# Two-layer hybrid decoder on one core: the memory's load, the pieces of the weight subtraction, and the order of layer 1's side work

## The chip, the cores and the metric

The kernel runs on one core of one Trainium2 chip. A core has five engines that work at the same time and wait for one another through semaphores: PE (TensorE, matrix products), DVE (VectorE), ACT (ScalarE), POOL (GpSimd) and SP (SyncE, which here only starts transfers). Transfers between main memory and the on-chip memory (SBUF) run on 16 DMA engines; SP and ACT each have a queue from which they are started in order. Products land in PSUM, a small second memory of eight banks. The metric is the device time of one execution in microseconds; lower is better. The number given for a kernel is the median of its runs.

## The reference

The input is x (512 tokens by 1024 channels) and a memory of 256 tokens. Each of two layers adds three things to x: a mixer, a cross-attention into the memory, and a gated feed-forward block with a short convolution. Only the mixers differ, and cut to what matters here they are:

```
layer 0:  xn = rmsnorm(h);  q, k, v, p = split(xn @ ev_w_in)
          a = block-sparse attention of 8 heads (q, k, v)
          b = per group g of 4: trailing mean of p over w = 2, 4, 8, 16 tokens, minus p, @ pool_w[g]
          h += concat(a, b) @ ev_w_out
layer 1:  z, qkv, gate, b_raw, a_raw = split(rmsnorm(h) @ od_w_in)
          u, v = split(gelu(z));  v = layernorm(v);  c = u * (tril(W) v + bias)      # spatial gate
          q, k, v = silu(short convolution of qkv), per head normed                  # 4 heads
          d = gated delta rule over chunks (triangular solve in a chunk, a scan over chunks)
          h += concat(c, d * silu(gate)) @ od_w_out
each:     mem_n = rmsnorm(mem);  k, v = split(mem_n @ wkv);  h += softmax(q k') v @ wo
          h += (silu(g) * up) @ down       # after a causal convolution of width 3
```

## The kernel before

x is held transposed, channels on the 128 partitions, as eight tiles of 128 by 512. Every product is made in three passes: both operands are split into a high part rounded to a shorter format and a low remainder, and PE adds high x high, high x low and low x high (`mm3`, lines 115 to 118). So a product of a 1024-deep weight block with 512 tokens is 8 k-steps of three matmuls.

**Weights.** `fetch` (line 120) starts a 512 KB transfer from SP's queue into one of three raw buffers. `wload` (line 125) makes the high part with a copy on ACT (line 108) and the low part, raw minus high, with one subtraction over all 1024 columns on POOL (line 109); the high parts have three buffers, the low parts two. So POOL can be one product ahead of PE and then waits until PE gives a buffer back. `parts=2` at the start lets the first three weights go in two halves, each a copy and a subtraction. In the last products of the kernel the subtraction is given to DVE (`sub=nc.vector`).

**Order of the work.** PE's order is written by hand in both mixers (`manual_schedule`), in layer 1 POOL's as well; elsewhere the framework orders the engines by its own estimate when the program is built. The tool for writing PE's order is a queue of generators: `later` appends work, and `fill(n)` lets PE do n units of it, a unit being one k-step of three matmuls with 512 columns (half a unit for the 256 tokens of the memory). `fill` stands wherever PE would otherwise wait for a chain on DVE or ACT. The amounts are the constants FILL_QT, FILL_AV, FILL_INV, FILL_LEV and FILL_SCAN at the top.

**Start.** `setup` (line 296) starts, on SP, the eight tiles of x with the first value weights between them, and on ACT's queue the gains and then, through `mem_load(0)` (line 527), the memory, 1 MB. ACT then makes the high part and the square of each tile of x (lines 111, 242 and 245), then the first weights' high parts, and PE begins with the value product, `proj_tok`, of 32 k-steps.

**Norms.** The scale of a token's row (rstd) is applied after the products. `norm_around` (line 258) makes two products; at the last k-step of the first it puts in the sums of squares, and before k-step 4 of the second the transposition of rstd to a row (`norm_row`, on PE at line 278). Between them lies a chain of tiny DVE steps, `rsqrt` (line 210). It is used in layer 0's mixer, layer 1's mixer and both feed-forward blocks.

**Layer 0's mixer.** For each of four pairs of heads, `attend` goes through four blocks of queries: scores, softmax on DVE and ACT, `fill(FILL_QT)` with 7 units, transposition of the probabilities (line 453). Then comes `fill(FILL_AV)`, and then the product with the values (line 473), which needs the low parts of the probabilities (ptl). The queue holds the later pairs' keys and queries, the memory's keys and values, and the four pooling groups. `pooled` (line 367) makes a trailing mean by doubling: per level a small copy of the head of the tile (line 373) and an addition over the rest (line 374), and then three steps for the result `po`, of which two (lines 379 and 380) cover only the first w columns. All are on DVE.

**Layer 1's mixer.** Projections with a short convolution (`conv_silu`, line 755: a multiplication, three taps on DVE, two steps on ACT) give keys, values and queries per head. A chain on DVE inverts triangular blocks in 31 steps of two instructions each (lines 998 and 1000), with `fill(FILL_INV)` after each step. The queue `stream` holds, in this order: keys 2 and 3, the gate with the split of the memory, the four values, the four queries, the memory's eight keys, its two value halves. A value or query is transposed by PE (`value_turn` with line 807, `query_turn` with line 817) at the third k-step of the item after the next one. After the inversion the inverse goes through main memory and back (lines 1006 and 1008, on SP), is completed in two levels of products, and the chunks are scanned (lines 1079 to 1127). The spatial gate's product (`od_wz`) is appended to the queue after the inversion; its layer norm, an `rsqrt` and four scalings (lines 1153 to 1158), stands behind the scan after `drain`, and PE's first spatial product (line 1171) needs it.

## Time and profile before

| | us |
|---|---|
| median of 3 runs | 1547.3 |
| lowest, highest run | 1546.19, 1548.87 |
| the profiled execution | 1547.88 |
| its span, first to last instruction | 1546.2 |
| PE busy in it | 1476.8 |
| DVE, ACT, POOL busy in it | 797.6, 631.6, 622.1 |

The times of a profile are those of one execution: its device time is 1.7 us above its span. A line of the profile that groups instructions reads: line of the kernel, engine, operation, the tile written and the tiles read, sizes, count, then busy time, mean duration in ns, and the idle time of that engine just before, with what ended it. A line of a timeline begins with the start and the duration in us, and in brackets stands how long the engine had been idle, and who released it. A line of the waits reads "engine line <- whom it waited for: total us, times, longest". In a table of stretches each engine has its busy time and, in brackets, its number of instructions; behind them stand PE's granted clock (1.00 is full speed), the share of the DMA engines and GB/s. PEld is PE's loading of weights into the array, which runs beside the matmuls; SPq and ACTq are the queues from which transfers are started.

### The profile page before, as it was taken

What the parts mean: (1) busy time and instruction counts of PE and PEld (TensorE: products, weight loads), DVE (VectorE), ACT (ScalarE), POOL (GpSimd) and SP (SyncE); (2) the same over time, 40 slices, a digit from 0 to 9 for tenths busy, and PEclk for the clock granted to TensorE, in tenths of its full rate; (3) what the DMA queues carried; (4) which work ended last, traced back from release to release, by engine and by line L of the source; (5) the groups of instructions that cost most, each with busy time, mean ns of one, the idle gap of its engine ahead of it and who ended that gap; (6) DMA issues with size and microseconds to landing.
All of it is one profiled execution on the core that took longest, in us unless ns stands there. A gap on an engine that the chain in (4) does not pass through costs nothing.

```text
span 1546.2 us, 18654 instructions
## 1 busy us (share of the span) xinstructions
PE 1476.8 (96%) x7105; PEld 1222.8 (79%) x7105; DVE 797.6 (52%) x1416; ACT 631.6 (41%) x990; POOL 622.1 (40%) x302
## 2 busy tenths in 40 slices
PE   4989899999999999999999899899999999999996
PEld 3767788788888888888777879787888888888886
DVE  3566664445552352355668824764455541542546
ACT  4456553343442342344553321354344432432444
POOL 3334344224444444444443462343233444444441
PEclk9999999999999999999999999999999999999998
DMA  5323243123333333333222341232123323323323
GB/s 170 85 83 91 85 136 97 55 57 96 96 95 96 96 92 100 97 93 112 82 75 89 102 140 46 75 86 79 55 84 94 97 87 104 96 77 114 95 86 114
DMA packets 48265, 143.33 MB, mean 93 GB/s; under 512 B 10032, under 2 KB 12848, under 8 KB 47920
## 3 DMA queue, kind: packets, MB, share of 16 engines
q1 hardware_dynamic: 44352, 137.71, 30.4%
q10 hardware_dynamic: 3824, 4.43, 0.9%
q8 instruction: 56, 0.92, 0.2%
q14 instruction: 33, 0.27, 0.1%
HBM read 139.50 MB, written 2.62 MB: 92 GB/s over the span
## 4 chain that ended last, share of the span: by engine, by line
PE 84%; DVE 10%; ACT 2%; issue 2%; DMA 1%; POOL 1%; DVEq 0%; SPq 0%; POOLq 0%; ACTq 0%
PE mm L116 24%; PE mm L118 24%; PE mm L117 24%; PE sc L118 1%; PE sc L116 1%; PE sc L117 1%; DVE sq L998 1%; DVE rsq_a L218 1%; POOL wl L109 1%; DVE lanes L1000 1%; DVE pt L763 1%; PE mm L142 1%; PE mm L145 1%; PE mm L143 1%; DVE rsq_b L220 1%
## 5 line engine op out<-in xcount | busy, mean ns | idle before, releaser
L109 POOL TENSOR_TENSOR wl<-wr,wh 128x1024 fp32r<-128x1024 f32 (+2 forms) x256 | 607.1, 2374 | 890.0 <-PE mm L118 799.7
L108 ACT CAST wh<-wr 128x1024 fp32r<-128x1024 f32 (+2 forms) x262 | 268.3, 1028 | 505.4 <-PE mm L117 266.9
L116 PE MATMUL mm<-xh,wh 128*128 128x512 f32 x1056 | 416.2, 394 | 0.3 <-DVE vv L112 0.3
L118 PE MATMUL mm<-xh,wl 128*128 128x512 f32 x1056 | 413.3, 391 | 0.0
L117 PE MATMUL mm<-xl,wh 128*128 128x512 f32 x1056 | 412.0, 390 | 0.0
L116 PEld LDWEIGHTS mm<-xh,wh 128*128 128x128 f32 x1056 | 199.1, 189 | 42.6 <-issue 2.1
L116 PE MATMUL mm<-ah,wh 128*128 128x512 f32 (+1 forms) x617 | 231.8, 376 | 0.0
L118 PEld LDWEIGHTS mm<-xh,wl 128*128 128x128 f32 x1056 | 198.7, 188 | 41.6
L117 PEld LDWEIGHTS mm<-xl,wh 128*128 128x128 f32 x1056 | 198.9, 188 | 40.7 <-issue 0.2
L118 PE MATMUL mm<-ah,wl 128*128 128x512 f32 (+1 forms) x617 | 230.8, 374 | 0.0
L117 PE MATMUL mm<-al,wh 128*128 128x512 f32 (+1 forms) x617 | 229.8, 373 | 0.2
L283 DVE TENSOR_TENSOR h<-h,mm 128x512 f32<-128x512 f32 x72 | 49.4, 687 | 179.1 <-PE mm L118 161.3
L117 PEld LDWEIGHTS mm<-al,wh 128*128 128x128 f32 x617 | 116.7, 189 | 22.7 <-DVE al L109 0.9
L118 PEld LDWEIGHTS mm<-ah,wl 128*128 128x128 f32 x617 | 116.6, 189 | 21.5
L116 PEld LDWEIGHTS mm<-ah,wh 128*128 128x128 f32 x617 | 116.8, 189 | 20.2 <-issue 0.2
L680 DVE TENSOR_TENSOR hf<-mm,acc 128x512 f32<-128x512 f32 x88 | 60.8, 691 | 133.5 <-PE mm L118 130.7
L112 DVE SCALAR_TENSOR_TENSOR xl<-h,gains,xh 128x512 fp32r<-128x512 f32 x48 | 68.8, 1435 | 41.5 <-ACT xh L111 41.3
L686 DVE SCALAR_TENSOR_TENSOR pt<-hf,cw,pt 128x511 f32<-128x511 f32 x88 | 66.3, 754 | 37.0 <-ACT pt L683 35.5
L686 DVE SCALAR_TENSOR_TENSOR sc<-hf,cw,sc 128x511 f32<-128x511 f32 x88 | 66.4, 754 | 35.4 <-ACT sc L683 33.5
L108 ACT CAST ah<-sg 128x512 fp32r<-128x512 f32 x44 | 27.3, 622 | 99.5 <-DVE sg L691 99.5
L690 ACT ACTIVATE sg<-pt 128x512 f32<-128x512 f32 x44 | 26.4, 599 | 70.2 <-DVE pt L686 70.2
L109 DVE TENSOR_TENSOR al<-sg,ah 128x512 fp32r<-128x512 f32 x44 | 30.5, 692 | 30.3 <-ACT ah L108 30.3
(344 smaller groups left out, 1777.0 us busy)
## 6 DMA issues: line engine op xcount, KB each, us to landing
wr<-in_up SPq DMA_DIRECT2D x88, 512.0 KB, 3.6
wr<-in_down SPq DMA_DIRECT2D x35, 448.0 KB, 3.3
wr<-in_xv SPq DMA_DIRECT2D x16, 512.0 KB, 3.7
wr<-in_xk SPq DMA_DIRECT2D x16, 512.0 KB, 3.6
wr<-in_xq SPq DMA_DIRECT2D x16, 512.0 KB, 3.5
wr<-in_xo SPq DMA_DIRECT2D x16, 512.0 KB, 3.6
wr<-in_down SPq DMA_DIRECT2D x16, 512.0 KB, 3.5
wr<-in_od_w SPq DMA_DIRECT2D x16, 512.0 KB, 3.6
```

The source lines that it names most:

```text
L108: nc.scalar.copy(h, src)
L109: (sub or nc.vector).tensor_sub(l, src, f32(h))
L112: nc.vector.scalar_tensor_tensor(l, src, scale, f32(h), op0=ALU.mult, op1=ALU.subtract)
L116: t.matmul(ps, lh, rh, start=start, stop=False)
L117: t.matmul(ps, lh, rl, start=False, stop=False)
L118: t.matmul(ps, ll, rh, start=False, stop=stop)
L142: t.matmul(ps, h[:, c], xh, start=k == 0, stop=False)
L143: t.matmul(ps, h[:, c], xl, start=False, stop=False)
L283: self.nc.vector.tensor_add(self.h[n], self.h[n], ps)
L680: nc.vector.tensor_mul(hf, ps, rb)
L686: nc.vector.scalar_tensor_tensor(y[:, sh:], hf[:, :S - sh], w[:, tap:tap + 1], y[:, sh:], op0=ALU.mult, op1=ALU.add)
L690: nc.scalar.activation(sg, ys[0], AF.Silu)
```

## The change

It has six parts.

1. `wload` first makes all copies on ACT and then subtracts in pieces of 256 columns, four for 1024, where POOL does it; on DVE it stays one piece.
2. `mem_load` starts its transfer on SP's queue instead of ACT's, in both layers, and for layer 0 it is called after the value product instead of in `setup`.
3. In `norm_around` the transposition of rstd moves from k-step 4 to k-step 6 of the second product. FILL_AV goes from 4 to 6.
4. In `pooled` the head copy of each level and the two steps over the first w columns go from DVE to POOL.
5. Layer 1's stream becomes: keys 2 and 3, the gate, then value and memory key by turns, query and memory key by turns, then the first half of the memory's values in four parts, each with a `query_key` behind it. The second half is appended behind the spatial gate's product.
6. The spatial gate's layer norm joins its product in one generator, `spatial`, which the queue goes through during the levels and the scan.

```diff
-FILL_AV = 4
+FILL_AV = 6
...
         for c in range(0, cols, cols // parts):
             q = slice(c, c + cols // parts)
-            self.split(h[:, q], l[:, q], raw[:, q], sub=sub or nc.gpsimd)
+            nc.scalar.copy(h[:, q], raw[:, q])
+        sub, w = (sub or nc.gpsimd), (M if sub is None else 2 * S)
+        for c in range(0, cols, w):
+            q = slice(c, min(c + w, cols))
+            sub.tensor_sub(l[:, q], raw[:, q], f32(h[:, q]))
...
-        ps = self.proj(srcs[0], xs, between={KT - 1: sums}), self.proj(srcs[1], xs, between={4: row})
+        ps = self.proj(srcs[0], xs, between={KT - 1: sums}), self.proj(srcs[1], xs, between={6: row})
...
-        self.mem_load(0)
...
             pv = self.proj_tok([i["ev_wv"][m] for m in range(4)], xs, raws=self.first,
                                banks=[self.sc(), self.sc(), self.mm(), self.mm()])
+            self.mem_load(0)
...
-                    nc.vector.tensor_copy(nx[:, :sh], cur[:, :sh])
+                    nc.gpsimd.tensor_copy(nx[:, :sh], cur[:, :sh])
...
-                nc.vector.tensor_mul(po[:, :w], cur[:, :w], icnt[:, :w])
-                nc.vector.tensor_sub(po[:, :w], po[:, :w], pf[:, :w])
+                nc.gpsimd.tensor_mul(po[:, :w], cur[:, :w], icnt[:, :w])
+                nc.gpsimd.tensor_sub(po[:, :w], po[:, :w], pf[:, :w])
...
-        self.nc.scalar.dma_start(self.mem_x, self.i["memT"])
+        self.nc.sync.dma_start(self.mem_x, self.i["memT"])
...
+                for posts in left:
+                    for post in posts:
+                        post()
+                        yield 0.5
...
-            self.later(stream(
-                [(key(2),), (key(3),), (gate_parts(),)] + [(value(hd), turn(value_turn, hd)) for hd in range(4)]
-                + [(query(hd), turn(query_turn, hd)) for hd in range(4)]
-                + [(mem_part("k", n),) for n in range(2)]
-                + [(mem_part("k", 2), turn(query_key, 0)), (mem_part("k", 3), turn(query_key, 1)),
-                   (mem_part("k", 4), turn(query_key, 2)), (mem_part("k", 5), turn(query_key, 3)),
-                   (mem_part("k", 6),), (mem_part("k", 7),), (mem_part("v", 0),), (mem_part("v", 1),)]))
+            items = [(key(2),), (key(3),), (gate_parts(),)]
+            for hd in range(4):
+                items += [(value(hd), turn(value_turn, hd)), (mem_part("k", hd),)]
+            for hd in range(4):
+                items += [(query(hd), turn(query_turn, hd)), (mem_part("k", 4 + hd),)]
+            for t in range(4):
+                items += [(rows(mem_part("v", 0), t), turn(query_key, t))]
+            self.later(stream(items))
...
-            self.later(self.proj_tok_gen([i["od_wz"][m] for m in range(4)], xs, TT, gelu_stats))
+            def spatial():
+                yield from self.proj_tok_gen([i["od_wz"][m] for m in range(4)], xs, TT, gelu_stats)
+                vv = self.tiny(4, "vv")
+                nc.vector.tensor_scalar(vv, mv[:, :, 1], EPS, None, op0=ALU.add)
+                rv = self.rsqrt(vv, 4, "rv")
+                for t in range(TT):
+                    zv = vns[t]
+                    nc.vector.tensor_scalar(zv, zv, mv[:, t, 0:1], rv[:, t:t + 1], op0=ALU.subtract, op1=ALU.mult)
+
+            self.later(spatial(), mem_part("v", 1))
```

(`rows(gen, t)` hands out the next four k-steps of one generator; the six lines of the layer norm behind `drain` go.)

More of the change, by code (lines that the diff above doesn't have):

```diff
@@ L863, in stream, with rows @@
                     left.append(posts)
+                for posts in left:
+                    for post in posts:
+                        post()
+                        yield 0.5
             turn = lambda f, *a: lambda: f(*a)
-            self.later(stream(
-                [(key(2),), (key(3),), (gate_parts(),)] + [(value(hd), turn(value_turn, hd)) for hd in range(4)]
-                + [(query(hd), turn(query_turn, hd)) for hd in range(4)]
-                + [(mem_part("k", n),) for n in range(2)]
-                + [(mem_part("k", 2), turn(query_key, 0)), (mem_part("k", 3), turn(query_key, 1)),
-                   (mem_part("k", 4), turn(query_key, 2)), (mem_part("k", 5), turn(query_key, 3)),
-                   (mem_part("k", 6),), (mem_part("k", 7),), (mem_part("v", 0),), (mem_part("v", 1),)]))
+            parts_of = {}
+            def rows(gen, t):
+                gen = parts_of.setdefault("v", gen)
+                for _ in range(4):
+                    u = next(gen, None)
+                    if u is None:
+                        return
+                    yield u
+            items = [(key(2),), (key(3),), (gate_parts(),)]
[6 more added lines that the diff above has]
+            self.later(stream(items))
             self.fill(8)
@@ L1152, in odd @@
             nc.scalar.dma_start(lnb, i["ln_b"].to_broadcast([P, 512]))
-            vv = self.tiny(4, "vv")
-            nc.vector.tensor_scalar(vv, mv[:, :, 1], EPS, None, op0=ALU.add)
-            rv = self.rsqrt(vv, 4, "rv")
-            for t in range(TT):
-                zv = vns[t]
-                nc.vector.tensor_scalar(zv, zv, mv[:, t, 0:1], rv[:, t:t + 1], op0=ALU.subtract, op1=ALU.mult)
             c_out = []
```

## The prediction

> **What bounds the kernel now.** I read four views in this order: the page, the waits of PE (TensorE), a table of stretches, and timelines around the longest waits.
>
> ```profile
> PE 1476.8 (96%) x7105; PEld 1222.8 (79%) x7105; DVE 797.6 (52%) x1416; ACT 631.6 (41%) x990; POOL 622.1 (40%) x302
> ```
>
> The span is 1546.2 us, so PE is without work for 69.4 us, and the change removes none of its 7105 matmuls. It can only win those 69.4 us and time in which PE's clock is down. Who PE waited for:
>
> ```profile
> PE sc L116 <- ACT wh L108: 19.4, 1, 19.4
> PE pt L453 <- ACT p L444: 9.5, 3, 4.9
> PE pt L278 <- DVE rstd L222: 6.8, 5, 2.5
> PE pt L817 <- ACT qT L765: 4.6, 1, 4.6
> PE sc L1171 <- DVE zt L1158: 4.0, 1, 4.0
> PE pt L807 <- ACT kf L765: 3.5, 1, 3.5
> PE mm L117 <- POOL wl L109: 2.7, 2, 1.6
> PE pt L252 <- DVE acc L246: 2.7, 1, 2.7
> PE sc L118 <- DVE xql L109: 2.5, 2, 1.3
> PE mm L473 <- DVE ptl L109: 1.4, 1, 1.4
> ```
>
> Columns: total, times, longest. A third is the start (19.4). The others are a few waits of 1 to 5 us, all in the mixers, the norms and the tail; the feed-forward stages have none. The clock beside them, by stretches (the last columns are granted clock, DMA share, GB/s):
>
> ```profile
> 4.00:14.00 10.00, 0.00 (x0) 0.00 (x0) 4.34 (x7) 4.96 (x8) 0.00 (x0) 1.00 1.00 357
> 80.00:100.00 20.00, 14.97 (x65) 11.52 (x64) 13.71 (x30) 12.04 (x23) 9.17 (x4) 0.83 0.24 79
> 180.00:200.00 20.00, 17.76 (x100) 14.23 (x101) 8.37 (x31) 14.74 (x32) 5.27 (x3) 0.84 0.29 82
> 500.00:520.00 20.00, 20.00 (x89) 16.45 (x88) 4.26 (x6) 4.81 (x6) 9.63 (x4) 1.00 0.30 86
> 860.00:880.00 20.00, 15.41 (x116) 15.29 (x115) 17.69 (x40) 8.89 (x14) 10.52 (x5) 0.83 0.31 101
> 980.00:1000.00 20.00, 15.97 (x76) 13.74 (x75) 14.76 (x31) 6.98 (x10) 6.39 (x3) 0.83 0.18 53
> 1520.00:1540.00 20.00, 14.19 (x114) 13.40 (x112) 14.83 (x43) 8.20 (x17) 1.89 (x2) 0.87 0.29 97
> ```
>
> An undisturbed stretch (500 to 520) does 89 matmuls of 512 columns in 20 us: 0.225 us each, 0.67 us for one k-step of three. The stretches with the waits of 4.0 to 4.9 us all have a granted clock of 0.83 or 0.84. A clock of 0.83 over 20 us is 2 x 0.17 x 20 = 6.8 us at half speed; what of it lies behind the wait slows real work:
>
> ```profile
> 96.18 0.63 PE L117 MATMUL mm<-wl,mh 128*128 128x512 f32 x1
> 96.60 0.63 PE L118 MATMUL mm<-wh,ml 128*128 128x512 f32 x1
> ```
>
> Here, 2 us after the 4.9 us wait, a matmul starts every 0.42 us instead of 0.225. If some 4 us of the 6.8 lie behind the wait, half of that, 2 us, is lost on top of the wait; I put 2 us on each of the long waits, and somewhat less on the 3.5 us one. The Trainium skill (TensorE: Matmul & The Clock Gate, Part 1) says that the clock falls after an idle window of about 3.4 us. The waits of 4.0 to 4.9 us agree; the stretch 1520 to 1540 has 0.87 with no wait above 2.7, so the trace does not bear it out as a sharp bound. By the rule a wait cut to 2.6 us costs no clock, by that stretch it may still cost 2 us; the sum below is that without, the bounds allow for the other.
>
> Why the waits are long shows in one mechanism:
>
> ```profile
> 84.79 2.42 POOL L109 TENSOR_TENSOR wl<-wr,wh 128x1024 fp32r<-128x1024 f32 x1 [2.03 <-ACT wh L108]
> 84.83 2.39 DVE L379 TENSOR_TENSOR po<-sq,icnt 128x2 f32<-128x2 f32 x1
> ```
> ```profile
> L379 DVE TENSOR_TENSOR po<-sq,icnt x4: 148/2332/2390, 84.8 to 205.9; 128x2 f32<-128x2 f32 x1, 128x4 f32<-128x4 f32 x1, 128x8 f32<-128x8 f32 x1, 128x16 f32<-128x16 f32 x1
> ```
> ```profile
> 174.44 2.67 DVE L377 SCALAR_TENSOR_TENSOR po<-sq,kf 128x504 f32<-128x504 f32 x1
> 177.03 2.31 DVE L379 TENSOR_TENSOR po<-sq,icnt 128x8 f32<-128x8 f32 x1
> ```
>
> A multiplication of two columns takes 2.39 us on DVE when it starts 0.04 us behind a POOL weight subtraction of 2.42 us, and 0.148 us at its best. DVE stands still until the whole POOL instruction is over. The second pair costs about 4 us of such standing just ahead of PE's wait at 182 us.
>
> **Part by part.** *Weight subtraction in four pieces.* POOL's rows:
>
> ```profile
> L109 POOL TENSOR_TENSOR wl<-wr,wh 128x1024 fp32r<-128x1024 f32 x221 | 536.8, 2430 | 788.0 <-PE mm L118 719.0 <-ACT wh L108 20.0 <-PE mm L117 10.6
> ```
> ```profile
> L109 POOL TENSOR_TENSOR wl<-wr,wh 128x512 fp32r<-128x512 f32 x6 | 7.9, 1344 | 20.9 <-ACT wh L108 16.8 <-PE mm L118 4.1
> ```
>
> Half the columns cost 1.34 instead of 2.43, so an instruction is about 0.26 us plus 2.1 ns a column, and a piece of 256 columns some 0.8 us (an estimate from these two rows; bounds: 0.61, a quarter of the whole, and 1.34). Four pieces take 3.2 us, 0.8 more than now. A product uses PE for 8 k-steps, 8 x 0.67 = 5.4 us, and POOL's 788 us of idle time, which PE ended, are the cover. If that cover is gone (memory keys, 2.8 us of PE each, below), POOL is 0.4 us a weight too slow; layer 0 has its eight keys in two runs of four, layer 1's second value half one of four weights: I charge 1 us. What a DVE instruction can lose at one meeting falls from 2.4 to 0.8. The Trainium skill (SBUF — State Buffer, two separate sides) calls the port pair of these engines an exclusive lock, held for the whole instruction. The rows agree. By the lock the term for layer 0's attention is that given below; if the two shared the bandwidth instead, the cut would leave DVE's share as it is, and the sum would be near the weak gain among the rivals.
>
> *Memory behind x.* Layer 0's memory leaves ACT's queue at the very start and goes on SP's queue behind the value weights.
>
> ```profile
> mv<-in_memT ACTq DMA_DIRECT2D x1, 1024.0 KB, 7.0
> ```
> ```profile
> 6.71 0.72 ACT L111 ACTIVATE xh<-h,gains 128x512 fp32r<-128x512 f32 x1 [3.47 <-DMA h<-in_xT]
> ...
> 16.48 0.71 ACT L111 ACTIVATE xh<-h,gains 128x512 fp32r<-128x512 f32 x1
> 17.09 0.61 ACT L245 ACTIVATE sq<-h 128x512 f32<-128x512 f32 x1
> 17.61 0.71 ACT L111 ACTIVATE xh<-h,gains 128x512 fp32r<-128x512 f32 x1
> ```
>
> From 4 to 14 us the DMA engines are full (share 1.00, 357 GB/s), so 1 MB less ahead of x is worth 1.05 MB / 357 GB/s = 2.9 us of transfers. ACT begins the first tile at 6.71 and the eighth at 17.61, 10.9 us later; where x is there already a tile takes 17.61 - 16.48 = 1.13 us, seven of them 7.9, so 3.0 us are waits for x. If the first tile lands where it does now, up to 2.9 of these go, and I put the lower bound at 2; if it comes earlier too, the transfers allow 2.9 and a shorter last stretch perhaps 1.5 more, 4.4. I take 3.2. On SP the memory stands ahead of the key weights of the first pair, which PE needs only after 32 k-steps (over 20 us), and its squares stand in ACT's queue there too: no charge. Layer 1's load just changes queue: nothing.
>
> *The row of scales two k-steps later, 4 to 6.* Of the five waits for rstd one is the tail's (2.5); four norms have 6.8 - 2.5 = 4.3. That is 1.1 on the mean, and two k-steps are 1.35 us of cover. I take all 4.3 (bounds 3.5 and 4.3). The consumers of the row get it at most 1.35 us later, with four PSUM banks in hand.
>
> *Layer 0's attention.* The three waits for p sum to 9.5: one of 4.9 and, of the 4.6 left, nearly all at 182. The small multiplications and subtractions at the head of the pooling groups go to POOL, so the 2.39 us at 84.83 leaves DVE's path: of 4.9 remain 2.6, and 2 us of clock come back. At 182 some 4 us of standing become one piece, 0.8: 3.4 of the 4.2 or so, and 2 us of clock. The added wait: DVE's next addition now needs POOL's little copy, and POOL may have four pieces queued ahead (0 to 3.2 us for each of ten levels); behind it on DVE stand the score reductions. PE has seven units of 0.67 us as cover; I charge 0.5 us. FILL_AV 4 to 6 adds two units, 1.35 us, in front of the wait for ptl (1.4). Sum: 2.3 + 2 + 3.4 + 2 - 0.5 + 1.4 = 10.6 (bounds 4 and 13).
>
> *Layer 1, the inversion.* Two waits (4.6 and 3.5) and about 3.5 us of clock are 11.6 in all. PE transposes a value or query tile some work after its convolution's product. Now that is one product and three k-steps; then it is one memory key and three. A key:
>
> ```profile
> 857.72 0.28 PE L118 MATMUL mm<-ah,wl 128*128 128x256 f32 x1
> 857.84 0.28 PE L116 MATMUL mm<-ah,wh 128*128 128x256 f32 x1
> ```
>
> 24 matmuls at 0.118 us are 2.8 us, so the lead falls from 5.4 + 2.0 = 7.4 to 4.8 us. The convolution's own latency, first DVE step to the end of its activation, quiet and loaded:
>
> ```profile
> 815.00 0.69 DVE L757 TENSOR_TENSOR kf<-mm,acc 128x512 f32<-128x512 f32 x1 [1.60 <-PE mm L118]
> ```
> ```profile
> 819.58 0.60 ACT L765 ACTIVATE kf<-pt 128x512 f32<-128x512 f32 x1 [3.12 <-DVE pt L763]
> ```
> ```profile
> 859.51 0.68 DVE L757 TENSOR_TENSOR kf<-mm,acc 128x512 f32<-128x512 f32 x1
> ```
> ```profile
> 864.06 0.60 ACT L765 ACTIVATE qT<-pt 128x512 f32<-128x512 f32 x1 [1.37 <-DVE pt L763]
> ```
>
> 5.2 us (815.00 to 820.18) and 5.2 (859.51 to 864.66); the last one only began late, because DVE (17.69 of 20 us busy) was behind. With a key between two convolutions DVE has 8.2 us of PE time for each instead of 5.4, so it should not fall behind; but 5.2 against 4.8 leaves a short wait, which I put at 0.8 us for each of eight turns, 6.4 us (bounds: nothing; 4.6 us each, as the late one). Gain 11.6 - 6.4 = 5.2. The two waits for weights (2.7) sit right behind, where now memory weights follow one another; I take half, 1.4.
>
> *Layer 1, the spatial gate.* Its statistics and scaling go from behind the scan into it: 4.0 and 2 us of clock go. They now stand in DVE's queue between the scan's steps, and the second half of the memory values fills the end; I charge 1.5 (bounds 0 and 4). Gain 4.5.
>
> *Elsewhere.* The waits for xql (2.5) follow DVE chains that meet POOL: 1.5 gained. The tail (2.7 and 2.5) stays.
>
> Sum: 3.2 + 4.3 + 10.6 + 5.2 + 1.4 + 4.5 + 1.5 - 1 = 29.7. The profiled execution took 1547.88, the median of the runs is 1547.3: 1547.9 - 29.7 = 1518.2, and 0.6 less against the median, so 1517.5.
>
> **The rivals.** *DVE keeps what it loses (weak gain).* If DVE, where it issues one port-bound step after another, waits for each of the four pieces in turn, it loses 3.2 us a weight instead of 2.4, and only what is moved counts: start 3.2, rows 4.3, half of attention 5, spatial 4, weights 1, and nothing from the inversion, where DVE's queue sets the pace: 17.5, or 1530. For it speaks DVE's load of 17.69 in 20; against it that convolution steps between need no such port.
>
> *The shorter lead (slower).* Place: the eight turns in the inversion. If each waits as the late one did, 4.6 and 2 us of clock, they cost 8 x 6.6 = 52.8 instead of 11.6: 24.5 from the rest less 41.2 is 16.7 slower, 1564. It decides from (24.5 + 11.6) / 8 = 4.5 us a turn. For it: that late turn had only a key and three half steps ahead of it, as the new ones nearly have. Against: half of DVE's load per PE time is gone.
>
> *Nothing.* The waits move by as much as they shrink: within 3 us, what a measurement of this kernel can tell from no change (0.2%).
>
> **How the numbers follow.** Forecast 0.66, its own range 1505 to 1528 from the bounds (inversion and attention both good: 12 us more; attention and start poor: 10 less). Weak gain 0.22, nothing 0.05, slower 0.05; 0.02 for a gain beyond the range. The range to hold 8 in 10 reaches to the weak gain: 1503 to 1537. Faster by over 0.2%: 0.66 + 0.22 + 0.02 = 0.90; within: 0.05; slower: 0.05.
>
> **What would show it.** Right: the first matmul near 16 us; no rstd wait but the tail's; L379 gone from DVE and no tiny DVE instruction above about 1 us; waits of p below 3 us; granted clock 1.00 in the stretches now at 0.83; waits at L807 and L817 short and many; none at L1171; POOL busy some 150 to 200 us more. Wrong: pieces of POOL well above 1 us, DVE in the inversion still full, turns of over 4 us each, or a first matmul still at 19.

## The result, and the profile after

The changed kernel takes 1512.38 us (median of four runs, 1509.75 to 1512.74); the kernel before took 1548.09 us beside it (1546.19 to 1551.95). The ratio is 0.9763, with a 95% interval of 0.974 to 0.9785. The forecast was 1517.5 us in a range of 1503 to 1537: a gain of 29.7 us foretold, 35.7 measured. The two numbers lie close together, but two terms of the sum missed by far, in opposite directions, and a third was met for another reason. That they come out so near is in part luck.

The profiled execution took 1512.74 us, its span is below. Line numbers are those of the changed kernel: up to the convolutions they are 4 higher than before (282 was 278, 457 was 453, 769 was 765, 811 was 807, 821 was 817), in the inversion 20 higher (997 was 977, 1018 was 998). Line 133 is the weight's copy on ACT, line 137 its subtraction on POOL. First the head of the page:

```profile
span 1510.7 us, 19479 instructions
...
PE 1471.7 (97%) x7105; PEld 1219.6 (81%) x7105; DVE 772.4 (51%) x1398; ACT 631.7 (42%) x990; POOL 779.0 (52%) x1076
```

PE is busy for 1471.7 us, 5 less than before; most of what went is its waiting. POOL is busy 157 us more (622.1 before), as forecast. What PE waits for (engine, tile, line, then the releaser; total, count, longest):

```profile
PE pt L457 <- ACT p L448: 7.6, 5, 3.5
PE sc L116 <- ACT xh L111: 5.5, 1, 5.5
PE pt L811 <- ACT kf L769: 5.2, 3, 2.7
PE pt L256 <- DVE acc L250: 2.7, 1, 2.7
PE sc L118 <- DVE xql L109: 2.5, 2, 1.3
PE pt L282 <- DVE rstd L226: 2.5, 1, 2.5
PE pt L1146 <- DVE vt L1128: 1.3, 1, 1.3
```

The first wait of the run, 19.4 us before, is 5.5. Four of the five waits for rstd are gone, so are the wait behind the scan and the waits for layer 1's weights. The waits for p went from 9.5 to 7.6 only, and one of 3.5 is left. The waits for kf at the value turns were one of 3.5 and are three of up to 2.7. The waits for xql stand as they stood.

The clock: in these traces PE runs at full or at half clock, and every spell of half clock ahead of the tail lasts 3.41 or 6.83 us. Before the change there are five, of 6.8, 6.8, 3.4, 6.8 and 6.8 us (at 91, 180, 838, 862 and 985 us), 30.7 in all, summed in the first line below. In the changed kernel three are left, 13.6 us in all:

```profile
sum 30.71, PE 20.62 PEld 18.49 DVE 21.17 ACT 14.59 POOL 2.23; mean PE 4.12 PEld 3.70 DVE 4.23 ACT 2.92 POOL 0.45
```
```profile
76.10:82.92 6.82, 5.94 (x18) 5.07 (x19) 1.77 (x5) 3.88 (x9) 2.03 (x4) 0.50 0.34 108
181.91:185.32 3.41, 3.41 (x19) 3.41 (x18) 1.57 (x4) 1.01 (x3) 2.13 (x5) 0.50 0.24 28
803.14:806.55 3.41, 2.83 (x9) 2.44 (x10) 3.01 (x9) 0.53 (x1) 0.00 (x0) 0.50 0.48 145
```

The first column is the stretch and its length, then PE's busy time; the column behind POOL's is the granted clock. The spells lie around the wait at 77 us, behind two waits at 180 us (1.7 and 0.9 us), and around the 2.7 us wait at 802 us. A matmul takes nearly twice its time there (0.42 us against 0.225 in the prediction's rows), so about half of what PE works in the spells is lost, an estimate from 20.62 us of work before and 12.18 now: 10.3 and 6.1 us.

Where the 35 us come from is read from when PE reaches the same instruction in both traces (first start in each; the gain is the difference of the stretch):

```
stretch, ending with                         before     after    gain
start, to the sums of the first norm          49.83     34.96    14.9
layer 0's attention, to cross-attention's
  first scores                               270.87    251.01     5.0
cross-attention, feed-forward, to the sums
  of layer 1's first norm                    745.35    724.56     0.9
to the inversion's first key product         796.68    774.05     1.8
inversion, to the first level product        906.50    874.84     9.0
levels and scan, to its last product         966.61    936.68    -1.7
spatial gate, to its last product           1005.56    971.05     4.6
the rest, to the last transposes           1538.97   1503.47     1.0
```

The inversion's stretch does not hold the same work: 548 matmuls run in it before and 539 in the changed kernel. Nine with 512 columns, 9 x 0.225 = 2.0 us, now stand behind the scan (173 and 181 matmuls in the spatial gate's stretch). For equal work the inversion's gain is 7.0 us and the spatial gate's 6.6.

### The profile page after: what moved, and what is told of

Its sections match the earlier page's. It is cut to its first block, busy times and chain, and to the rows that moved or that the text cites. A ratio compares the mean times of both kernels' runs of the same rounds, so it can differ in the third digit from the quotient of the medians.

```text
span 1510.7 us, 19479 instructions
## 1 busy us (share of the span) xinstructions
PE 1471.7 (97%) x7105; PEld 1219.6 (81%) x7105; DVE 772.4 (51%) x1398; ACT 631.7 (42%) x990; POOL 779.0 (52%) x1076
## 4 chain that ended last, share of the span: by engine, by line
PE 89%; DVE 6%; ACT 2%; POOL 1%; DMA 1%; issue 1%; DVEq 0%; SPq 0%; POOLq 0%; ACTq 0%
PE mm L116 26%; PE mm L118 26%; PE mm L117 26%; PE sc L116 1%; PE sc L118 1%; PE sc L117 1%; POOL wl L137 1%; PE mm L146 1%; PE mm L149 1%; PE mm L147 1%; DVE pt L767 1%; PE pt L646 1%; PE pt L457 1%; PE mm L477 0%; PE sc L1075 0%
## 5 line engine op out<-in xcount | busy, mean ns | idle before, releaser
L137 POOL TENSOR_TENSOR wl<-wr,wh 128x256 fp32r<-128x256 f32 x1012 | 756.0, 779 | 697.4 <-PE mm L118 603.0
L112 DVE SCALAR_TENSOR_TENSOR xl<-h,gains,xh 128x512 fp32r<-128x512 f32 x48 | 46.7, 972 | 41.2 <-ACT xh L111 41.1
L250 DVE TENSOR_TENSOR acc<-acc,sq 128x512 f32<-128x512 f32 (+1 forms) x52 | 54.3, 1044 | 3.3 <-ACT sq L249 3.1
```

Of the source, the lines that this page charges most:

```text
L112: nc.vector.scalar_tensor_tensor(l, src, scale, f32(h), op0=ALU.mult, op1=ALU.subtract)
L137: sub.tensor_sub(l[:, q], raw[:, q], f32(h[:, q]))
L250: nc.vector.tensor_add(acc, acc, sq)
```

## Experiments

The theory on trial is the prediction's: each part of the change removes a wait of its own, pieces shorten what a DVE step can lose, and the new order of layer 1's products keeps its turns short. Against it stand, for the start, that something other than the transfers moved, and for layer 1, that the pieces did it and not the order. All times below are medians of four runs; a ratio is to the kernel before, run beside it. Undoing one part is told against the changed kernel's 1512.4.

**Layer 0's memory ahead of x again.** Edit: `self.mem_load(0)` back in the setup, on ACT's queue.

> The changed kernel with one part undone: layer 0's memory goes out again on ACT's queue at the very start, ahead of x (and layer 1's load on that queue too). Theory 'order': the memory's place decides when ACT makes the first weight casts; with the memory ahead ACT does all eight x tiles first, the first matmul is back near 19.4 us and the kernel takes about 14 us more, 1526. Rival 'copies first' (the new form of the weight load brought the casts forward): the first matmul stays below 9 us and only the transfers' 3 us come back, 1515 to 1516.

1526.2 us, ratio 0.9856 (0.984 to 0.9872): 13.8 us lost, as the theory 'order' had it. PE's first matmul in this kernel:

```profile
18.23 0.80 PE L116 MATMUL sc<-wh,xh 128*128 128x512 f32 x1 [18.23 <-ACT wh L133]
```

**ACT's order at the start written out.** The memory stays behind x, but the first block takes ACT's order by hand: the eight tiles of x with their squares, then the first casts, as before the change.

```diff
+            hand = ExitStack()
+            hand.enter_context(tc.manual_schedule(engines={PE, Activation}))
             self.norm_begin(self.gain(0))
...
+            hand.close()
+            st.enter_context(tc.manual_schedule(engines={PE}))
             self.mem_load(0)
```

> The changed kernel with the memory where the change put it, behind x, but ACT's order at the start written out as it was before: all eight x tiles with their squares, then the casts of the first value weights. Theory 'order': only the transfers' part of the start is left, the first matmul comes at 16 to 17 us, 11 us later than in the changed kernel, 1523 to 1524. Rival 'transfers' (the megabyte ahead of x was what held the start): the first matmul comes before 9 us whatever ACT does first, and the time is within 4 us of 1512.

1526.0 us, ratio 0.9854 (0.9836 to 0.9872): 13.6 us lost, nearly all of it at the start, with the megabyte out of x's way. ACT and PE in this kernel:

```profile
15.49 0.61 ACT L249 ACTIVATE sq<-h 128x512 f32<-128x512 f32 x1
16.01 1.64 ACT L133 CAST wh<-wr 128x512 fp32r<-128x512 f32 x3
```
```profile
16.66 0.79 PE L116 MATMUL sc<-wh,xh 128*128 128x512 f32 x1 [16.66 <-ACT wh L133]
```

and in the changed kernel:

```profile
3.91 0.62 ACT L133 CAST wh<-wr 128x512 fp32r<-128x512 f32 x1 [1.16 <-DMA wr<-in_ev_wv]
4.68 0.72 ACT L111 ACTIVATE xh<-h,gains 128x512 fp32r<-128x512 f32 x1 [0.16 <-DMA h<-in_xT]
...
6.59 0.62 ACT L133 CAST wh<-wr 128x512 fp32r<-128x512 f32 x1 [0.67 <-DMA wr<-in_ev_wv]
```
```profile
5.45 0.80 PE L116 MATMUL sc<-wh,xh 128*128 128x512 f32 x1 [5.45 <-ACT xh L111]
```

With the casts behind all of x PE's first matmul waits for ACT's seventeenth instruction, although its weight landed long before; with a cast ahead of each early tile it waits for two. That order is not in the code: PE's alone is written out in this block, the framework orders ACT's instructions when the kernel is built, and it chose otherwise once the memory's transfer no longer stood ahead of x; by what estimate, no run shows. The first matmul comes at 18.23 to 19.40 with the memory ahead, at 16.66 with the transfer moved alone, at 5.45 with the order that came with it: 1.6 to 2.7 us for the transfer and 11.2 for the order. Of the transfer's part little reaches the end: mem_ahead and act_order, which both have ACT's old order, differ by 0.2 us in their medians and by 1.3 at the first norm's sums (49.0 and 47.7 us).

**One piece.** Edit: `(M if sub is None else 2 * S)` to `2 * S`.

> The changed kernel with each weight's subtraction in one POOL instruction again (copies still ahead of it). Theory 'lock' (DVE stands while a POOL instruction runs, so the length of one counts): DVE instructions of over 2 us come back, the waits for p and kf in front of PE grow, about 8 us more, 1520 (layer 0's attention 4, inversion 2, elsewhere 2). Rival 'DVE keeps what it loses': pieces change no sum, within 3 us of 1512. Rival 'pieces cost POOL': faster by 1 to 3 us, 1510.

1524.8 us, ratio 0.9846 (0.9831 to 0.9861): 12.4 us lost. Of these 3.2 lie at the start, ahead of the first norm's sums, and 9 in the inversion; layer 0's attention is 1.5 us *shorter* with one piece (below).

**Two pieces.** Edit: the same width to `S`, 512 columns.

> The changed kernel with two POOL pieces of 512 columns instead of four of 256. Theory 'lock, by length': the loss lies between one piece (1524.8) and four (1512.4), at a third of the way, 1516 to 1517. Rival 'POOL's fixed cost' (two pieces leave POOL 0.3 to 0.5 us a weight that four take, and POOL is late in the runs of keys): 1511 to 1512.

1519.9 us, ratio 0.9826 (0.9811 to 0.984): 7.6 lost, between one piece and four. The loss grows with the length of a POOL instruction, but not in proportion: 7.6 of the 12.4 are there at half the length, nearly all of it in the inversion (7.2 us in the profile). What halving one piece gains, 4.8 us, is for the most part the start (3.1 us in the profile).

**The pieces alone**, in the kernel before.

> The kernel before with one part of the change alone: a weight's subtraction in four POOL pieces behind its copies. Theory 'lock' (what a DVE step loses at a meeting is one POOL instruction): most of the 12.4 us that one piece cost in the changed kernel, without the 3.2 of its start, which needs early casts: 9 us less than before, 1539, in layer 0's attention and in the inversion. Rival 'DVE keeps what it loses': within 3 us of 1548.

1532.9 us, ratio 0.9911 (0.9896 to 0.9926): 14.2 us gained, 5 more than expected. Of them 6.8 are in layer 0's attention, 4.4 in the inversion, and the wait of 4.0 us for the spatial gate fell to three of 2.1 in all, with no other part of the change:

```profile
PE sc L1175 <- DVE zt L1162: 2.1, 3, 1.3
```

What the pieces do is not quite what the forecast or its rival said. Four groups of DVE steps, first in the kernel before, then in the changed one:

```profile
L112 DVE SCALAR_TENSOR_TENSOR xl<-h,gains,xh 128x512 fp32r<-128x512 f32 x48 | 68.8, 1435 | 41.5 <-ACT xh L111 41.3
L246 DVE TENSOR_TENSOR acc<-acc,sq 128x512 f32<-128x512 f32 (+1 forms) x52 | 37.0, 711 | 2.6 <-ACT sq L245 2.6
L998 DVE TENSOR_TENSOR sq<-lanes 64x31 f32<-64x31 f32 (+15 forms) x31 | 18.4, 592 | 0.4
L1000 DVE TENSOR_TENSOR lanes<-lanes,sq 64x31 f32<-64x31 f32 (+15 forms) x31 | 16.8, 543 | 0.6
```
```profile
L250 DVE TENSOR_TENSOR acc<-acc,sq 128x512 f32<-128x512 f32 (+1 forms) x52 | 54.3, 1044 | 3.3 <-ACT sq L249 3.1
L1020 DVE TENSOR_TENSOR lanes<-lanes,sq 64x31 f32<-64x31 f32 (+15 forms) x31 | 14.5, 467 | 0.9
L112 DVE SCALAR_TENSOR_TENSOR xl<-h,gains,xh 128x512 fp32r<-128x512 f32 x48 | 46.7, 972 | 41.2 <-ACT xh L111 41.1
L1018 DVE TENSOR_TENSOR sq<-lanes 64x31 f32<-64x31 f32 (+15 forms) x31 | 13.9, 449 | 2.6 <-DMA lanes<-da 2.0
```

The splits of x are 22 us shorter in all, but the sums of squares, which follow them, are 17 longer: 105.8 us together before, 101.0 after. The inversion's own steps went from 35.2 to 28.4. In these groups DVE keeps most of what it lost, in more and smaller parts, as the rival had it. Over the whole kernel the sum falls by more: DVE is busy for 797.6 us before and for 771.3 with the pieces alone, by the same 1416 instructions; in the changed kernel it is 772.4, with two pieces 801.2 and with one 803.4. The longest step falls too. One step of 175 columns in the kernel before, and one of 247 in the changed one:

```profile
827.09 2.54 DVE L998 TENSOR_TENSOR sq<-lanes 64x175 f32<-64x175 f32 x1
829.66 0.33 DVE L1000 TENSOR_TENSOR lanes<-lanes,sq 64x175 f32<-64x175 f32 x1
```
```profile
814.60 0.40 DVE L1018 TENSOR_TENSOR sq<-lanes 64x247 f32<-64x247 f32 x1
815.04 0.82 DVE L1020 TENSOR_TENSOR lanes<-lanes,sq 64x247 f32<-64x247 f32 x1
```

0.33 becomes 2.54 when a whole weight is in its way (POOL's subtraction began at 827.03 us and took 2.40), 0.40 becomes 0.82 with a piece. Whether the longest step counts or the sum of what DVE loses, the kernel with two pieces tells, in the inversion: one piece, two and four, with the busy times of PE, PEld and DVE behind the stretch's length:

```profile
775.84:885.52 109.68, 96.73 (x538) 82.95 (x537) 82.37 (x152) 40.20 (x56) 54.85 (x29) 0.95 0.39 112
774.19:882.14 107.95, 96.36 (x538) 82.30 (x537) 79.88 (x153) 40.09 (x56) 58.51 (x50) 0.95 0.40 111
774.05:874.84 100.79, 93.37 (x539) 80.24 (x537) 72.39 (x153) 40.18 (x56) 65.71 (x91) 0.98 0.41 114
```

The longest DVE step in this stretch is 2.47 us with one piece, 1.40 with two and 1.16 with four. With two pieces DVE's busy time falls by only 2.5 us, and the stretch by 1.7; with four it falls by 7.5 more, and the stretch by 7.2. So here the time goes with what DVE loses in sum, and a shorter longest step is worth little while the sum stays. A limit would fit these three as well (a step of 1.4 us still outlasts the products that PE has in front of it, one of 1.2 does not), and no run parts the two. In layer 0's attention the time does not follow the sum: there four pieces take 11 us from DVE's 126.8, and the stretch is no shorter. Why quarters lower the sum and halves do not, no run shows.

**The pooling groups' small steps on DVE again.** Edit: `nc.gpsimd` to `nc.vector` for the copies, the multiplication and the subtraction.

> The changed kernel with the small copies, the multiplication and the subtraction of the pooling groups on DVE again (12 to 13 instructions). Theory of the prediction (a small DVE instruction can stand a whole POOL instruction, now 0.75 us): about 2 us more than the changed kernel, 1514, seen in the waits near 77 and 182 us. Rival 'POOL's queue holds the chain': the copies wait for weight pieces queued ahead of them on POOL, so DVE does them sooner: 2 to 4 us less, 1509, the 3.5 us wait at 77 us shorter.

1508.0 us, ratio 0.9738 (0.9723 to 0.9753): 4.4 us *faster* than the changed kernel, the rival's side and size, though not its place: the gain is at 182 us, and the wait at 77 grew to 5.3. DVE in the changed kernel, and POOL beside it:

```profile
175.28 0.69 DVE L378 TENSOR_TENSOR sq<-kf 128x511 f32<-128x511 f32 x1
178.12 0.69 DVE L378 TENSOR_TENSOR sq<-sq 128x510 f32<-128x510 f32 x1 [2.15 <-POOL sq L377]
178.73 0.15 DVE L447 RECIPROCAL rs<-sm 128x1 f32<-128x1 f32 x1
```
```profile
174.61 3.35 POOL L137 TENSOR_TENSOR wl<-wr,wh 128x256 fp32r<-128x256 f32 x4 [6.74 <-PE mm L118]
177.91 0.19 POOL L377 COPY sq<-kf 128x1 f32<-128x1 f32 x1
178.15 2.29 POOL L377 COPY sq<-sq 128x2 f32<-128x2 f32 x3
```

A copy of one column waits behind four pieces of a weight; DVE's next addition waits 2.15 us for the copy, and the reciprocal of the attention's sums, which PE needs, stands behind that addition on DVE. With the copies on DVE the same reciprocal ends 2.5 us sooner:

```profile
176.24 0.15 DVE L447 RECIPROCAL rs<-sm 128x1 f32<-128x1 f32 x1
```

**The row of scales at k-step 4 and the filler at 4 units again.**

> The changed kernel with the row of scales back at k-step 4 and the filler behind the attention back at 4 units. Terms of the prediction: 4.3 us for the row (about 1.1 at each of four norms) and 1.4 for the filler: 1518, with four more waits for rstd. Rival 'only the rows' (the wait behind the filler is set by the chain of POOL and DVE, which ends no earlier): 1516.5. Rival 'neither' (with pieces the chain of rstd is short): 1512.

1516.1 us, ratio 0.9801 (0.9785 to 0.9817): 3.8 lost, the rival 'only the rows'. The waits for rstd are back; without the tail's 2.9, the longest, they are 3.6 us at four norms:

```profile
PE pt L282 <- DVE rstd L226: 6.5, 5, 2.9
```

From the first norm's sums to cross-attention's scores this kernel is 1.1 us *shorter*, a wait for the row included. The filler does cover its wait (1.0 us for ptl is back, and PE is idle for 9.95 us instead of 8.75), but PE works 3.4 us of this stage at half clock instead of 9.4, and that outweighs it. In time the two units gained nothing.

**Layer 1's products in the old order.** The stream of before, with the spatial gate left in the scan and the second half of the memory values behind it.

> The changed kernel with layer 1's order of products as it was: four values, four queries, then the memory keys (the spatial gate stays inside the scan, the second half of the memory values behind it). Theory of the prediction (the interleaving saves 5.2 us of turns and 1.4 of weights): 6 to 7 us more, 1519, with long waits for kf and for the weights behind the queries. Rival 'the pieces did it' (the waits went because DVE was no longer held, not because of the order): within 2 us of 1512.

1512.6 us (1509.7 to 1514.9), ratio 0.9758 (0.9735 to 0.978): no difference that these runs can tell. Its inversion has long waits at the query turns and for weights,

```profile
PE pt L821 <- ACT qT L769: 5.2, 2, 3.6
PE mm L117 <- POOL wl L137: 2.5, 2, 2.0
```

against 5.2 at the value turns in the changed kernel. In the profiles the stretch from the first key product to the first level product shows how order and pieces depend on each other:

```
from first key product to first level product, us
                                  one piece     four pieces
old order (before, pieces alone)    109.8          105.4
old order, values' second half moved  -            103.6
new order (one piece, changed)      109.7          100.8
```

The first row holds the nine matmuls, 2.0 us, that the other two have moved behind the scan. For equal work the new order by itself costs 1.9 us there; with the pieces it gives 2.8 in the profile. Five other kernels with four pieces and the values and queries in the new order (mem_ahead, act_order, pool_on_dve, old_rows, gate_behind) take 100.9 to 102.7. The medians, which scatter over 3 to 5 us, show 0.2. So it is worth 0 to 3 us, and more than that is not settled.

**The spatial gate behind the scan again.** Edit: the scaling back behind `self.drain()`.

> The changed kernel with the scaling of the spatial gate behind the scan again. Theory of the prediction (the wait behind the scan returns, and costs clock): 3 to 4.5 us more, 1516, of which a part comes back inside the scan, whose wait for vt gets shorter. Rival 'it was the pieces' (the chain of small DVE steps is short once no POOL instruction holds it): within 1 us of 1512.

1513.9 us, ratio 0.9773 (0.9753 to 0.9792): 1.6 us lost, between the two theories, with runs that overlap the changed kernel's (1512.5 to 1515.4 against 1509.8 to 1512.7). The wait of 4.0 us does not come back; in its place stand two of 0.8 in all, while the scan's 1.3 us wait for vt goes. In the profile only 0.8 us lies in the stages that the edit touches, the rest in the inversion (102.7 against 100.8), which it does not touch. From the first level product to the sums of the next norm, lines for before, pieces alone, this kernel and the changed one:

```profile
906.50:1060.85 154.35, 150.26 (x824) 129.92 (x823) 90.06 (x166) 51.29 (x75) 53.85 (x22) 0.98 0.27 78
893.92:1047.38 153.46, 151.33 (x824) 130.27 (x823) 87.30 (x166) 52.22 (x75) 72.35 (x88) 0.98 0.27 80
876.86:1028.87 152.01, 150.93 (x832) 129.52 (x833) 93.39 (x170) 51.26 (x74) 70.31 (x87) 1.00 0.26 80
874.84:1026.08 151.24, 149.93 (x832) 129.29 (x833) 94.65 (x170) 51.37 (x74) 70.27 (x86) 1.00 0.27 80
```

The last two hold the nine matmuls more, 2.0 us. For equal work the stretch is 5.1 us shorter than before: 0.9 by the pieces, 0.8 by the scaling's move, and 3.4 that come with the rest of the change. A likely cause is the memory values behind the gate's product, which give PE work while DVE scales; no run takes them out alone, so that is not shown.

**The value turns one product later**, besides the pooling steps on DVE. Edit: `(value(hd),), (mem_part("k", hd), turn(value_turn, hd))`.

> The pooling groups' small steps on DVE (1508.0 in its own run) and, besides, each value's transposes one product later, so that a memory key, a whole convolution product and three half steps lie in front of them instead of a key and three steps. Theory 'lead' (the turns wait because the lead is shorter than the convolution's latency): their three waits, 5.8 us, and 1 to 2 us of clock go, 1501 to 1502. Rival 'DVE behind' (the convolutions run late as a whole): the waits turn up at the query turns or the query keys, 1506 to 1508.

1507.1 us, ratio 0.9728 (0.9711 to 0.9746): 0.9 us less than without it, not 6; by its time the rival 'DVE behind', though the waits did not move on to the query turns. With twice the lead the value turns still wait:

```profile
PE pt L811 <- ACT kf L769: 5.3, 2, 3.7
```

**Layer 0's memory split spread over one more product**, besides that. Edit: `[step(rms), mixed(kq_gens(1)[1], parts, 4), mixed(pool_gen(0), parts, 4), ...]`, where the last number says behind every how many k-steps a part comes; it was every second, from the pooling product on.

> As late_turns, and the splitting of layer 0's memory (DVE and ACT steps between PE's filler products) spread over one product more, so that fewer DVE steps stand ahead of the attention's splits at 63 to 75 us. Theory 'DVE's queue' (the wait of 5.3 us for p at 77 us comes from memory steps ahead of the scores on DVE): that wait falls below 3 us and the half clock behind it goes, 4 us less than late_turns, 1497 to 1498. Rival 'the attention's own chain': the wait stays, within 1 us of late_turns.

1503.9 us, ratio 0.9705 (0.9687 to 0.9723): 3.3 us less than late_turns. The long wait for p at 77 us is gone, and a new one has come for the memory's own scales, which are now wanted too early:

```profile
PE pt L282 <- DVE mem_r L548: 2.3, 1, 2.3
...
PE pt L457 <- ACT p L448: 1.6, 4, 0.6
```

So the wait at 77 us came from DVE's queue, in which steps of the memory's split stood ahead of the attention's. What else is missing to the expectation is not taken apart; the new wait, with a spell of half clock behind it, and the turns, which keep 4.6 us, are what the trace has.

**The best found.** Pooling steps on DVE; the memory split spread, its row behind the whole query product; layer 1's four values one after another, and two memory keys behind each query, with its turn behind both.

```diff
-            plan = [[step(rms)] + kq_gens(1)[1:] + [mixed(pool_gen(0), parts), mixed(mem_part("v", 0), parts)],
+            plan = [[step(rms), mixed(kq_gens(1)[1], parts, (7,)), mixed(pool_gen(0), parts, (3, 7)),
+                     mixed(mem_part("v", 0), parts, (1, 3))],
...
-                items += [(value(hd), turn(value_turn, hd)), (mem_part("k", hd),)]
+                items += [(value(hd), turn(value_turn, hd))]
...
-                items += [(query(hd), turn(query_turn, hd)), (mem_part("k", 4 + hd),)]
+                items += [(query(hd),), (mem_part("k", 2 * hd), turn(query_turn, hd)),
+                          (mem_part("k", 2 * hd + 1),)]
```

(the last number of `mixed` names the k-steps behind which a part comes)

> The steps of the pooling groups on DVE; layer 0's memory split spread over more products, its row behind the whole query product; layer 1's four values one after another as before the change, and two memory keys behind each query, the query's transposes behind both. Theory 'DVE's queue': no wait for p above 1 us, the wait for the memory's row (2.3 us in spread_memory) gone, the waits at the value turns below 2 us in all, no waits at the query turns: 1498 to 1500. Rival 'the work only moves' (DVE is the pace in the inversion, and a wait returns at the turns or the query keys): 1503 to 1505.

1495.4 us (1495.2 to 1495.7), ratio 0.9667 (0.9652 to 0.9681): 17 us under the changed kernel and 3 better than expected. The inversion's stretch is 94.0 us against 100.8, and:

```profile
PE pt L457 <- ACT p L448: 3.3, 6, 0.9
...
PE pt L811 <- ACT kf L769: 0.5, 1, 0.5
```
```profile
800.00:820.00 20.00, 19.46 (x137) 17.90 (x135) 19.55 (x33) 9.52 (x14) 17.87 (x21) 1.00 0.43 128
```

DVE is busy for 19.55 of these 20 us and PE waits for almost nothing: what the products need is then done earlier or later than what the inversion needs. A full DVE is not the bound as long as its order suits PE. The inversion's 6.1 us against spread_memory (100.1) come with the keys behind the queries and none between the values; one run made both moves, so it does not tell which counts more.

## Why the prediction was right, and where its steps were wrong

*The direction and the range* were right; the total came out 6 us better, from errors that partly cancel.

*Memory behind x: 3.2 us forecast, bounds 2 to 4.4; 13.8 measured by undoing it.* The step that failed is "If the first tile lands where it does now, up to 2.9 of these go": the working took ACT's order of before as given, first all of x, then the casts, and priced the transfer alone. The transfer brought the first matmul forward by 1.6 to 2.7 us, but the kernel's time by only 0.2 (mem_ahead against act_order). The 11.2 us behind it are ACT's new order, shown by act_order. The prediction's own sign for this step, a first matmul near 16 us, is met by act_order alone.

*The row two k-steps later: 4.3 forecast.* All four waits are gone; undone, 3.6 us of waits come back, and 3.8 of time with the filler undone beside it.

*Layer 0's attention: 10.6 forecast, 5.0 measured*, a wait of 1.0 for the norm's row among them. Three steps failed. The largest is the clock: 2 us at each of the two long waits were to come back, and none did. PE works 9.4 us of this stage at half clock, against 7.8 before: the spell at 180 us is half as long as it was, but two waits of 1.7 and 0.9 us still bring one on, and the spell at 77 us is as long as that at 91 was. "I charge 0.5 us" for the wait of DVE's additions on POOL's little copies: it is 4.4, by the very mechanism that stands there (four pieces queued ahead, the reductions behind it on DVE). And of the first long wait for p (4.9 at 91 us before, now at 77) half was to go with the 2.39 us step: it fell to 3.5, since steps of the memory's split on DVE hold it, as spread_memory shows. The 3.4 us for the second pair do not need the move to POOL: pieces alone cut that wait from 4.2 to 0.9, with one of 1.3 further on, and gain 6.8 us in this stage. In the changed kernel that wait is gone, but three at later transposes are new (0.9, 1.7 and 0.9). From the first norm's sums to cross-attention's scores:

```
                         before  changed  one piece  pieces alone  pooling on DVE   best
stretch, us               221.0    216.0      214.5         214.2           211.3  206.1
of it PE idle              13.5      8.7       10.0          10.6             7.7    4.2
PE busy at half clock       7.8      9.4        4.1           2.8             4.1    0.0
```

So moving the small steps away and cutting the pieces are two cures for one ill, and together they take longer than either. Beside the pieces the move adds 1.0 us of idle time and 5.3 us of work at half clock (pooling on DVE against changed); beside the move the pieces save 1.2 us of idle time, and the 5.3 us at half clock outweigh it (one piece against changed). That is in the main why undoing the parts singly gives 27 us (13.8 + 12.4 + 3.8 + 1.6 + 0.2 - 4.4) and not 35.7: in this stage either cure can be taken out without a loss.

*Inversion and weights: 5.2 and 1.4 forecast, 7.0 measured for equal work* (9.0 with the nine matmuls that left the stretch). The size is near, by luck: the reason was wrong. The forecast gave it to the interleaving of keys and convolutions ("With a key between two convolutions DVE has 8.2 us of PE time for each"); the order costs 1.9 us without the pieces and gives at most 3 with them; with the order as it is, the four pieces are worth 8.9. The turns, put at 0.8 us each, cost more at the values (5.2 us in three waits, against 3.2) and nothing at the queries (against 3.2). The shorter lead did not decide: late_turns doubled it for 0.9 us.

*The spatial gate: 4.5 forecast; for equal work 6.6 in its stretch, less 1.7 in the scan, 4.9.* The wait and its half clock did go, but the scaling's move, to which the forecast gave this, is worth 0.8 in the profile and 1.6 at most; the pieces gave 0.9, the rest came with the other parts.

*Elsewhere 1.5 forecast, nothing measured:* both waits for xql stand at 1.3. *Pieces slower on POOL, 1 us:* four pieces take 4 x 0.74 = 3.0 us against 3.2 forecast, and no weight is late.

*The clock.* The forecast counted 9.5 us of clock (2 and 2 in attention, 3.5 in the inversion, 2 at the gate). PE's busy time, which holds what half clock adds, fell by 5.1 in all; by the spells (half of PE's work in them, an estimate) 4.2 came back: about 2.5 in the inversion, 2.6 at the gate, and 0.8 lost in attention. What failed is the sum's choice that a wait cut to 2.6 us or so costs no clock; the working had named the other case and left it to the bounds. The 3.41 us ahead of the spell at 803 us:

```profile
799.73:803.14 3.41, 1.31 (x6) 0.75 (x4) 3.36 (x8) 0.59 (x3) 2.35 (x4) 1.00 0.58 162
```

The Trainium skill (TensorE: Matmul & The Clock Gate, Part 1) puts the fall behind an idle window of about 3.4 us; the wait of 2.7 us does not reach that, PE works for 1.31 us of these 3.41, and here it was enough. The measurement decides: a wait of 2.7 us can bring half clock on in this kernel (one of 2.3 did in spread_memory), and where a wait shrank its spell kept its length or lost half of it, and did not go.

*The rivals.* "DVE keeps what it loses" holds for two pieces (801.2 us of DVE against 803.4) and not for four (772.4), and the gain it denied is there: 14.2 us by the pieces alone. The Trainium skill (SBUF — State Buffer, two separate sides) calls the port pair an exclusive lock for a whole instruction; the 2.54 us step above agrees. That each step of a run of DVE steps may meet a piece of its own, as the rival argued, is seen in the sums of squares, which got longer; over the whole kernel it did not decide. "The shorter lead" did not happen, no turn waits above 2.7 us. "Nothing" did not either.

## What to carry to other kernels

When a scheduler orders an engine's queue, moving one transfer can reorder work that the edit does not touch: ask in what order each engine will reach the first thing that the bounding engine waits for, before pricing bytes. Where two engines hold each other up, try more than one length of the long instruction, and count the busy time of the engine that waits beside its longest step: here halves shortened the longest step and left the sum, and only quarters lowered both and paid in the inversion. Don't also move small steps of a chain into the queue of the engine with the long instructions. A wait that is only shortened may keep its spell of half clock; count the clock as won where the wait goes. Before reading a gain from a stretch, count the instructions in it on both sides. An engine that is full for 20 us need not be the bound; place the filler so that what it must finish for the bounding engine comes first.

## What the runs showed of the hardware that was not expected

Pieces and DVE steps hold each other up, in both directions. Where DVE has one step with two inputs behind another, POOL's pieces of 0.74 us (the median) take 0.94, and some of DVE's steps of 0.40 take 0.82:

```profile
814.57 1.88 POOL L137 TENSOR_TENSOR wl<-wr,wh 128x256 fp32r<-128x256 f32 x2
```

A sum of squares, 0.71 us on the mean before, takes 1.04 with pieces. And the clock fell not only at the wait of 2.7 us but behind two of 1.7 and 0.9 us close together (0.50 from 181.91 to 185.32 us), and came back after 3.41 or 6.83 us each time.
